# Hybrid decoder layer: SSM and compression products on column tiles, the second gate on VectorE, and the front half as 190 tasks in a new order

## Chip, core and metric

The kernel runs on one core of a Trainium2 chip. The metric is the device time of one execution in microseconds; of several runs the median counts.

## What is computed

A decoder layer over 512 positions of width 1024, all in float32. A modulation vector in six parts (shift, scale and gate of two halves) comes from the condition `c`. The first half projects the normalised, modulated input at once into an attention part and an SSM part. The attention has 8 query heads and 2 key/value heads and three branches: compressed blocks, selected blocks, a window. The second half is a gated feed-forward layer with a causal convolution of three taps.

```python
mod = silu(c) @ w_ada + b_ada
sh1, sc1, gt1, sh2, sc2, gt2 = split(mod, 6)
h = rmsnorm(x, norm1_g) * (1 + sc1) + sh1
zq, zkc, zvc, zks, zvs, zkw, zvw, zg, zs = split(h @ w_in)
# compressed keys and values: 31 blocks of 32 positions, flattened to 2048
kc = gelu((blocks(rope(zkc)) + pe_k) @ w_ck1) @ w_ck2
vc = gelu((blocks(zvc) + pe_v) @ w_cv1) @ w_cv2
o_attn = g0 * softmax(q kc) vc + g1 * selected(q, ks, vs) + g2 * window(q, kw, vw)
y = gelu(Re(C scan(B zs)) + D zs);  y_ssm = y * sigmoid(y @ w_glu + b_glu)
x = x + gt1 * (concat(rmsnorm(o_attn), rmsnorm(y_ssm)) @ w_o)
h = rmsnorm(x, norm2_g) * (1 + sc2) + sh2
a, v = split(conv3(h @ w_up));  x = x + gt2 * ((silu(a) * v) @ w_down)
return rmsnorm(x, normf_g)
```

## The kernel before

The work goes through in this order: modulation and SSM constants; the transposed, modulated input; the SSM projection (`zs`); keys (`zk`) and values (`zv`); the compression; queries (`zq`); the attention, with the SSM's outputs woven in; the output projection (`os`, `oa`); the up projection with the convolution (`up`, 22 pairs of column blocks); the down projection (`dn`).

**Large products** are made of float32 values that are split into a high and a low part of the type fp32r. `mm3` (L111) multiplies high by high, high by low, low by high, which are the lines L112, L113 and L114 of the profile. A weight tile comes by DMA into one of the few `raw` buffers (128x1024, 512 KB); `weights` (L102) has its high part copied (a cast, `cpy`, L55 on ScalarE, L58 on VectorE) and its low part subtracted (L100, on VectorE or GpSimd). When both are done the `raw` buffer is free for the next load. Small products are plain float32; the profile shows two records for each.

**Modulation.** `ada_cols` (L307) computes 256 columns of `silu(c) @ w_ada`: eight products of 256 columns (L314), one on each of four column tiles of 32, twice over, with `csz` as weights, the condition in column 0 of 32 and zeros beside it. A copy brings the four partial rows to a tile `row..`, and two products with ones (L319) turn it into columns. The parts are called `ma`, `mp` (first half), `mg` (gates), `mb`, `mc` (second half). `gate_row` (L330) turns the columns of a gate into a row on all partitions by eight transposes (L336).

**Compression.** `hidden` (L763) builds the blocks `AM` in the tile `mid` and multiplies: 16 steps of 128, two halves of the 256 hidden units, so 32 products for the keys (`w_ck`), then 32 for the values (`w_cv`). The hidden units stand in the output's partitions:

```python
PE.matmul(ph[n][:, :62], r[:, m * 256 + n * 128:m * 256 + (n + 1) * 128],
          AM[:, mm].rearrange("p g n -> p (g n)"), start=mm == 0, stop=mm == 15)
```

Weight tiles go through the `raw` buffers, four for each kind. `compress` (L779) applies gelu and the second product (`co`), once for each kind.

**Attention.** `attend` (L850) goes through 16 units (four blocks of 128 queries, two key heads, two pairs of heads): scores `sc` (L876), masked maximum on VectorE (`mp`, `mx`, L890), exponential on ScalarE (`Ss`, L895), scaling; then the transposes of the compressed probabilities (`pc`, L909), their split `pz`, their product with the compressed values `VC` (L913), and for each key chunk transposes (`p`, L919), split (`pt`, L100) and four products (L929). All products of a unit add up in one bank `pv`.

**What sets the order.** The Python code issues the instructions in a hand-written order; a scheduler that simulates a timeline then orders each engine's queue from it. Each engine works its queue in order. A table `PICK` names for each copy, split and tile the engine or the pool that it goes to (`kn`). All loads are issued by SyncE, in its own queue: a load that waits for its buffer holds up those behind it.

## Time and profile before

| | us |
|---|---|
| three runs | 814.92, 819.27, 820.35 |
| median | 819.27 |
| profiled execution | 818.85 |
| its span | 817.1 |
| TensorE busy | 748.5 (92%) |
| VectorE busy | 469.2 (57%) |
| ScalarE busy | 320.3 (39%) |
| GpSimd busy | 269.2 (33%) |
| mean granted clock of TensorE | 0.936 |

The span is the profiled execution from its first to its last instruction; 1.75 us of that run's own time lie around it. The granted clock is a share of full speed: 1.0 is 2.4 GHz, 0.5 is 1.2 GHz, and a value between is a mean over a stretch. Busy shares are means over stages with different limits.

### The profile page before, as it was taken

The page shows a single profiled execution, that of the slowest core. Times are in us where ns is not written, and L with a number is a line of the kernel's source. Part 1 is how long each engine was busy: PE and PEld are TensorE (multiplying, and loading weights), DVE is VectorE, ACT ScalarE, POOL GpSimd, SP SyncE. Part 2 cuts the span into 40 slices and gives each one's busy share as a digit, 9 for nine tenths or more (in the row PEclk, how much of TensorE's full clock was granted, in tenths as well). Part 3 has the DMA queues.
Part 4 walks back from the last instruction along what each step waited for, and adds up shares of the span by engine and source line. Part 5 has one row for each costly group of instructions (what it writes and reads, how often), then busy time and mean ns, then how long its engine had stood idle before and what let it go on. Part 6 is the DMA issues. An engine that isn't in the chain of part 4 may idle for free.

```text
span 817.1 us, 11305 instructions
## 1 busy us (share of the span) xinstructions
PE 748.5 (92%) x4105; PEld 604.9 (74%) x4105; DVE 469.2 (57%) x1100; ACT 320.3 (39%) x659; POOL 269.2 (33%) x309
## 2 busy tenths in 40 slices
PE   2889989899679889989989999999999999999994
PEld 1469777787456768877779887878778888888883
DVE  5324464348789689778866555455545564132347
ACT  3543243101467767536433233333333322232223
POOL 4899559574522352474321000100000011300003
PEclk9889998759959999999989999999999999999997
DMA  8843226762101005200044133243324323223102
GB/s 298 313 162 105 100 66 209 251 218 73 41 16 23 9 1 222 89 1 1 6 155 155 52 103 109 98 155 103 129 80 153 103 90 114 93 90 104 52 0 103
DMA packets 30458, 86.72 MB, mean 106 GB/s; under 512 B 8295, under 2 KB 8739, under 8 KB 30371
## 3 DMA queue, kind: packets, MB, share of 16 engines
q1 hardware_dynamic: 30403, 86.00, 31.7%
q8 instruction: 32, 0.52, 0.3%
q14 instruction: 23, 0.19, 0.1%
HBM read 82.71 MB, written 2.10 MB: 104 GB/s over the span
## 4 chain that ended last, share of the span: by engine, by line
PE 76%; DVE 12%; ACT 4%; DMA 3%; POOL 2%; issue 2%; SPq 1%; POOLq 0%; DVEq 0%; ACTq 0%
PE up L112 9%; PE up L114 9%; PE up L113 9%; PE dn L114 5%; PE dn L112 5%; PE dn L113 5%; PE hid L776 2%; PE pv L929 2%; DVE Ss L890 2%; PE sc L876 1%; PE eup L113 1%; PE eup L112 1%; DMA adaa<-in_w_ada_dram 1%; PE eup L114 1%; PE p L919 1%
## 5 line engine op out<-in xcount | busy, mean ns | idle before, releaser
L112 PE MATMUL up<-h2h,uup 128*128 128x512 f32 x320 | 128.0, 400 | 0.0
L113 PE MATMUL up<-h2l,uup 128*128 128x512 f32 x320 | 125.8, 393 | 0.0
L114 PE MATMUL up<-h2h,uup 128*128 128x512 f32 x320 | 125.5, 393 | 0.0
L1223 DVE SCALAR_TENSOR_TENSOR us<-up,gt,us 128x511 f32<-128x511 f32 x80 | 59.9, 749 | 58.7 <-ACT us L1219 57.2
L1219 ACT ACTIVATE us<-up,gt 128x512 f32<-128x512 f32 x40 | 31.2, 780 | 109.5 <-PE up L114 109.5
L112 PEld LDWEIGHTS up<-h2h,uup 128*128 128x128 f32 x320 | 60.0, 188 | 15.9 <-ACT us L1219 1.6
L114 PEld LDWEIGHTS up<-h2h,uup 128*128 128x128 f32 x320 | 60.0, 188 | 15.0
L113 PEld LDWEIGHTS up<-h2l,uup 128*128 128x128 f32 x320 | 60.1, 188 | 13.4
L113 PE MATMUL dn<-udn,ghs 128*128 128x512 f32 x176 | 69.6, 396 | 0.0
L112 PE MATMUL dn<-udn,ghs 128*128 128x512 f32 x176 | 69.5, 396 | 0.0
L114 PE MATMUL dn<-udn,ghs 128*128 128x512 f32 x176 | 69.4, 396 | 0.0
L100 DVE TENSOR_TENSOR uup<-rup,uup 128x1024 fp32r<-128x1024 f32 x40 | 48.7, 1221 | 33.8 <-ACT uup L55 33.8
L100 POOL TENSOR_TENSOR udn<-rdn,udn 128x1024 fp32r<-128x1024 f32 x4 | 9.6, 2398 | 151.6 <-DVE udn L58 151.6
L64 POOL TENSOR_SCALAR Ss<-Ss,sm 128x384 f32<-128x384 f32 (+3 forms) x43 | 24.6, 588 | 52.1 <-DVE sm L899 30.1
L55 ACT ACTIVATE uup<-rup 128x1024 fp32r<-128x1024 f32 x36 | 37.8, 1050 | 4.8 <-DMA rup<-in_w_up_dram 3.3
L114 PEld LDWEIGHTS dn<-udn,ghs 128*128 128x128 f32 x176 | 33.1, 188 | 8.1
L112 PEld LDWEIGHTS dn<-udn,ghs 128*128 128x128 f32 x176 | 33.1, 188 | 8.0
L113 PEld LDWEIGHTS dn<-udn,ghs 128*128 128x128 f32 x176 | 33.1, 188 | 7.9
L876 PE MATMUL sc<-KS,QS 128*128 128x288 f32 (+2 forms) x128 | 33.2, 367 | 3.7 <-DVE mp L890 2.6
L929 PE MATMUL pv<-pt,VT 128*128 128x256 f32 x160 | 34.3, 326 | 0.9 <-DVE pt L100 0.9
L895 ACT ACTIVATE Ss<-Ss,mx 128x128 f32<-128x128 f32 (+3 forms) x64 | 35.1, 550 | 0.0
L1276 POOL TENSOR_TENSOR xr<-xr,nf 128x512 f32<-128x512 f32 x4 | 5.7, 1421 | 85.1 <-ACT jz L1275 85.1
(469 smaller groups left out, 1767.9 us busy)
## 6 DMA issues: line engine op xcount, KB each, us to landing
rup<-in_w_up_dram SPq DMA_DIRECT2D x44, 512.0 KB, 3.4
rdn<-in_w_down_dram SPq DMA_DIRECT2D x22, 512.0 KB, 3.3
mid<-in_w_ada_dram SPq DMA_DIRECT2D x16, 512.0 KB, 4.0
adaa<-in_w_ada_dram SPq DMA_DIRECT2D x8, 512.0 KB, 5.6
adap<-in_w_ada_dram SPq DMA_DIRECT2D x8, 512.0 KB, 5.5
adag<-in_w_ada_dram SPq DMA_DIRECT2D x8, 512.0 KB
adab<-in_w_ada_dram SPq DMA_DIRECT2D x7, 512.0 KB, 4.8
xt<-in_x_dram SPq DMA_DIRECT2D x4, 512.0 KB, 5.8
```

The lines of the kernel that those rows point to most:

```text
L55: A.activation(dst, src, AF.Copy, **({} if s is None else {"scale": s}))
L64: P.tensor_scalar(dst, src, s, 1.0, op0=ALU.mult, op1=ALU.mult)
L100: eng.tensor_tensor(out=lo, in0=src, in1=f(hi), op=ALU.subtract)
L112: PE.matmul(ps, w[0], m[0], start=start, stop=False)
L113: PE.matmul(ps, w[0], m[1], start=False, stop=False)
L114: PE.matmul(ps, w[1], m[0], start=False, stop=stop)
L776: PE.matmul(ph[n][:, :62], r[:, m * 256 + n * 128:m * 256 + (n + 1) * 128], AM[:, mm].rearrange("p g n -> p (g n)"), start=mm == 0, stop=m ...
L876: PE.matmul(ps[:, :n], QS[:, h, qs], KS[:, g, x, c0:c0 + n], start=x == 0, stop=x == 1)
L895: A.activation(Sv[:, br, :nk], Sv[:, br, :nk], AF.Exp, bias=mx[:, e, 1 + br:2 + br], scale=0.125, accum_out=sm[:, e, 1 + br:2 + br])
L929: PE.matmul(po[:, :256], VT[:, kc, br, g], pT[:, x, br * 256:(br + 1) * 256], start=False, stop=kc == qt and br == 1 and x == 1)
L1219: A.activation(u_[:, e * n:(e + 1) * n], p, AF.Identity, bias=cv[:, 3, c_:c_ + 1], scale=cv[:, 2, c_:c_ + 1])
L1223: V.scalar_tensor_tensor(o, p[:, :o.shape[1]], cv[:, 2 - d, c_:c_ + 1], o, op0=ALU.mult, op1=ALU.add)
```

## The change

The code of the front half, up to the up projection, is cut into 190 named tasks (`@task`, `@per`), which run in the order of a table `ORDER`. The scores and softmax of an attention unit (`S..`) and its products (`O..`) are tasks of their own. Beside that:

- The hidden products of the compression hold the blocks as weights (64 columns) and move the 256 columns of `w_ck1` or `w_cv1`; keys and values stand on the two column halves of the array and share one bank. Two transposes bring the hidden units back to partitions, gelu and copies run once for both kinds. `w_ck2` and `w_cv2` have a tile of their own.
- The compressed probabilities of a unit are one 128x128 tile with one transpose; their product with `VC` is four products of 128 columns and stands behind the first key chunk's products.
- The second gate (`g2`) and one quarter of `mc` (`c2`) are summed on VectorE: eight operations on 128x256, one scaled by each element of the condition. For the gate the bias is added to one row, and one product with ones adds up the partitions and writes the row to all of them; the columns and transposes are gone.
- `csz` is replaced by a broadcast of `cs` with a scale of 1/32 in the copy.
- The sum of squares of the SSM output is four products of 512 columns on four column tiles, a copy, and four one-column products, where 16 one-column products stood.
- Copies and splits are assigned anew, among them the up projection's: ScalarE 36 to 28 casts, GpSimd 2 to 6 casts and 0 to 8 low halves, VectorE 40 to 32 low halves. Several modulation weights come into other pools than `raw`.

```diff
-    def hidden(kind, w1, pe):
-        AM = mid[:, 2048:3040].rearrange("p (m g n) -> p m g n", m=16, g=2)
...
-                for n in range(2):
-                    PE.matmul(ph[n][:, :62], r[:, m * 256 + n * 128:m * 256 + (n + 1) * 128],
-                              AM[:, mm].rearrange("p g n -> p (g n)"), start=mm == 0, stop=mm == 15)
+    @per("hid", 0, 1, 2, 3)
+    def _(q):
...
+        for w1 in ("w_ck1", "w_cv1"):
+            rr.append(raw(f"{w1}{q}"))
+            nc.sync.dma_start(rr[-1], i[w1][q])
+        for m in range(4):
+            for kind in range(2):
+                PE.matmul(v.ph[kind * 64:(kind + 1) * 64, :256], v.AM[:, kind, q * 4 + m].rearrange("p g n -> p (g n)"),
+                          rr[kind][:, m * 256:(m + 1) * 256], start=v.nh == 1 and m == 0, stop=v.nh == 4 and m == 3)
...
+        if kn("ada_" + name, "PE", "V") == "V":
+            for k in range(KO):
+                w, ck = rr[k // 4][:, (k % 4) * 256:(k % 4 + 1) * 256], cs[:, k:k + 1]
+                if k == 0:
+                    V.tensor_scalar(row, w, ck, None, op0=ALU.mult)
+                else:
+                    V.scalar_tensor_tensor(row, w, ck, row, op0=ALU.mult, op1=ALU.add)
+            return row, ps
...
+    def gate2(jj):
+        row, ps = ada_sums(5120 + jj * 256, f"g2{jj}", raw)
+        c = slice(jj * 256, (jj + 1) * 256)
+        V.tensor_tensor(out=row[0:1], in0=row[0:1], in1=gt2[0:1, 0, c], op=ALU.add)
+        PE.matmul(ps[:, 256:512], bc(ones, (0, 128)), row, start=True, stop=True)
+        cpy(kn(f"e_gc{jj}", "A", "V"), gt2[:, 0, c], ps[:, 256:512])
...
-                for e in range(2):
-                    PE.transpose(pc_[:32, e * 128:(e + 1) * 128], sc[:, e], ident)
-                for x in range(2):
-                    PE.matmul(po[:, :256], VC[:, g], pT[:, x], start=x == 0, stop=False)
+        PE.transpose(pc_[:, :128], scz[ui], ident)
...
+            if kc == 0:
+                for e in range(2):
+                    for x in range(2):
+                        PE.matmul(po[:, e * 128:(e + 1) * 128], VC[:, g, e], pz[:, x], start=False,
+                                  stop=qt == 0 and e == 1 and x == 1)
...
-    for t in range(NT):
-        for ct in range(4):
-            PE.matmul(sq_ps[:, t:t + 1], sqs[:, ct, t * 128:(t + 1) * 128], ones[:, :1], start=ct == 0, stop=ct == 3)
+        for ct in range(4):
+            PE.matmul(sq_ps[32 * ct:32 * ct + 32], bc(ones, (0, 32)), v.sqs[:, ct], start=True, stop=True, tile_position=(0, 32 * ct))
+        sqr = sw("sqr")
+        cpy(kn("e_sqr", "A", "V"), sqr, sq_ps, 1.0 / 32)
+        for t in range(NT):
+            PE.matmul(sq_ps[:, t:t + 1], sqr[:, t * 128:(t + 1) * 128], ones, start=True, stop=True)
```

The order on TensorE in the compression, before: from the last products with the key weights into those with the value weights (`w_cv_1427` to `w_cv_1457` are the four loads).

```order
L776 MATMUL hid_1383<-mid,w_ck_1414 128x62
L776 MATMUL hid_1382<-mid,w_ck_1414 128x62
L776 MATMUL hid_1383<-mid,w_ck_1414 128x62
L314 MATMUL mg_1702<-mid,csz 32x256 x8
L776 MATMUL hid_1425<-mid,w_cv_1427 128x62 x4
L776 MATMUL hid_1425<-mid,w_cv_1437 128x62 x4
L776 MATMUL hid_1425<-mid,w_cv_1447 128x62 x2
L776 MATMUL hid_1426<-mid,w_cv_1427 128x62 x4
L776 MATMUL hid_1426<-mid,w_cv_1437 128x62 x4
L776 MATMUL hid_1426<-mid,w_cv_1447 128x62 x2
```

After: from the column sums of a gate (`mg`) over modulation products of the second half (`mb`) to the first products with the second pair of weights (`w_ck_1423`, `w_cv_1425`).

```order
L394 MATMUL mg_1268<-ones,rowg_1269 128x1 x2
L385 MATMUL mb_1285<-mid,cs 32x256 x4
L385 MATMUL mb_1285<-adab_1283,cs 32x256 x4
L394 MATMUL mb_1285<-ones,rowb_1286 128x1 x2
L744 MATMUL hid<-w_ck_1423,mid 64x256
L385 MATMUL mb_1363<-adab_1359,cs 32x256 x4
L385 MATMUL mb_1363<-adab_1361,cs 32x256 x4
L744 MATMUL hid<-w_cv_1425,mid 64x256
L744 MATMUL hid<-w_ck_1423,mid 64x256
L744 MATMUL hid<-w_cv_1425,mid 64x256
```

The value products no longer form a block of their own, and the products of each pair stand behind the load of that pair.

SyncE's queue at the same place, before (`mid` loads are modulation weights):

```order
L294 DMA mid<-in_w_ada_dram 128x1024 x3
L772 DMA w_ck_1394<-in_w_ck_dram 128x1024
L772 DMA w_ck_1404<-in_w_ck_dram 128x1024
L772 DMA w_ck_1414<-in_w_ck_dram 128x1024
L772 DMA w_cv_1427<-in_w_cv_dram 128x1024
L772 DMA w_cv_1437<-in_w_cv_dram 128x1024
L772 DMA w_cv_1447<-in_w_cv_dram 128x1024
L772 DMA w_cv_1457<-in_w_cv_dram 128x1024
L294 DMA mid<-in_w_ada_dram 128x1024 x2
L106 DMA rinq_1494<-in_w_in_dram 128x1024
L106 DMA rinq_1499<-in_w_in_dram 128x1024
L106 DMA rinq_1504<-in_w_in_dram 128x1024
```

After:

```order
L370 DMA mid<-in_w_ada_dram 128x1024 x6
L741 DMA w_ck_1423<-in_w_ck_dram 128x1024
L741 DMA w_cv_1425<-in_w_cv_dram 128x1024
L370 DMA mid<-in_w_ada_dram 128x1024
L741 DMA w_ck_1435<-in_w_ck_dram 128x1024
L741 DMA w_cv_1437<-in_w_cv_dram 128x1024
L741 DMA w_ck_1447<-in_w_ck_dram 128x1024
L741 DMA w_cv_1449<-in_w_cv_dram 128x1024
L370 DMA mid<-in_w_ada_dram 128x1024 x2
L115 DMA rinq_1488<-in_w_in_dram 128x1024
L115 DMA rinq_1493<-in_w_in_dram 128x1024
L115 DMA rinq_1498<-in_w_in_dram 128x1024
```

Before, the key tiles are requested one behind the other; after, a key and a value tile alternate, the first pair (`w_ck_1411`, `w_cv_1413`) is requested before these rows, and the others wait each for the read of an earlier tile.

TensorE in the attention, before, at the first products of unit 2748 (`pv_2748`; `sc` and `p` belong to its neighbours too):

```order
L929 MATMUL pv_2544<-pt_2558,VT 128x256 x3
L929 MATMUL pv_2544<-pt_2572,VT 128x256 x4
L919 MATMUL p_2757<-ident,Ss 128x128
L919 MATMUL p_2769<-ident,Ss 128x128 x4
L1071 MATMUL yT_2346<-ident,Y_1869 128x64 x8
L876 MATMUL sc_2964<-KS,QS 128x512 x2
L913 MATMUL pv_2748<-pz_2752,VC 128x256 x2
L929 MATMUL pv_2748<-pt_2762,VT 128x256
L876 MATMUL sc_3034<-KS,QS 128x288 x2
```

After, at the first products of unit 2944:

```order
L874 MATMUL pc_2945<-ident,scz_103 128x128
L832 MATMUL sc_3111<-KS,QS 128x512 x2
L832 MATMUL sc_3181<-KS,QS 128x288 x2
L892 MATMUL pv_2944<-pt_2955,VT 128x256 x4
L897 MATMUL pv_2944<-pz_2947,VC 128x128 x4
L892 MATMUL pv_2944<-pt_2971,VT 128x256
L882 MATMUL p_2978<-ident,Ss 128x128 x4
L892 MATMUL pv_2944<-pt_2971,VT 128x256 x3
```

The product with `VC` has moved from the first to the fifth place of its unit.

## Rows read from the trace of the kernel before

**Rows 1.** The page of the profiled execution: the busy time of each engine with its share of the span, and the shares of the chain that ended last.

```profile
PE 748.5 (92%) x4105; PEld 604.9 (74%) x4105; DVE 469.2 (57%) x1100; ACT 320.3 (39%) x659; POOL 269.2 (33%) x309
...
PE 76%; DVE 12%; ACT 4%; DMA 3%; POOL 2%; issue 2%; SPq 1%; POOLq 0%; DVEq 0%; ACTq 0%
```

**Rows 2.** Table of stretches of the span (start and end in us, length, then the busy time and the instructions of each engine, the granted clock of TensorE, the share of the DMA engines and their rate).

```profile
core 0: us, PE busy (x) PEld busy (x) DVE busy (x) ACT busy (x) POOL busy (x), PEclk, DMA share, GB/s
...
144.00:180.00 36.00, 31.88 (x214) 27.92 (x214) 15.51 (x30) 3.31 (x13) 23.09 (x34) 0.63 0.68 224
...
153.00:184.00 31.00, 28.50 (x139) 24.50 (x140) 14.62 (x25) 2.60 (x10) 20.48 (x16) 0.51 0.65 218
...
180.00:260.00 80.00, 67.90 (x458) 50.59 (x456) 64.67 (x263) 37.33 (x129) 33.15 (x30) 0.82 0.19 53
...
260.00:440.00 180.00, 165.46 (x997) 137.87 (x995) 143.61 (x459) 102.31 (x249) 76.21 (x80) 0.94 0.21 71
...
440.00:698.00 258.00, 258.00 (x1197) 207.26 (x1196) 130.97 (x162) 86.45 (x109) 15.46 (x9) 1.00 0.31 104
```

**Rows 3.** Timeline of TensorE in the compression stage (start, length, line, operation, tiles and shape, number of instructions in a row; in brackets the idle time ahead of it and what ended it).

```profile
143.54 1.89 PE L776 MATMUL hid<-mid,w_ck 128*128 128x62 f32 x16
...
146.09 1.07 PE L314 MATMUL mb<-adab,csz 128*32 128x256 f32 x16
...
147.48 2.00 PE L776 MATMUL hid<-mid,w_ck 128*128 128x62 f32 x16 [0.32 <-DMA w_ck<-in_w_ck_dram]
...
149.73 1.98 PE L776 MATMUL hid<-mid,w_ck 128*128 128x62 f32 x16
...
153.83 3.67 PE L776 MATMUL hid<-mid,w_ck 128*128 128x62 f32 x16 [2.12 <-DMA w_ck<-in_w_ck_dram]
...
159.56 13.91 PE L776 MATMUL hid<-mid,w_cv 128*128 128x62 f32 x64 [0.18 <-DVE mid L767]
...
179.49 0.80 PE L112 MATMUL zq<-uinq,hh 128*128 128x512 f32 x1
```

**Rows 4.** DMA issues between 112 and 185 us (size, and the median time from issue to landing).

```profile
w_ck<-in_w_ck_dram SPq DMA_DIRECT2D x4, 512.0 KB, 6.3
...
rinq<-in_w_in_dram SPq DMA_DIRECT2D x4, 512.0 KB, 4.4
```

**Rows 5.** Groups of instructions by line over the whole span: the low halves of the query weights on GpSimd, and the products and transposes of the compressed branch on TensorE (busy time in us, mean of one in ns, and behind the second bar the idle time ahead of them and what ended it).

```profile
L100 POOL TENSOR_TENSOR uinq<-rinq,uinq 128x1024 fp32r<-128x1024 f32 x4 | 10.0, 2489 | 4.2 <-PE hid L776 2.4 <-issue 1.1 <-DVE KS L792 0.7
...
L913 PE MATMUL pv<-pz,VC 32*128 32x256 f32 x32 | 9.2, 355 | 6.5 <-ACT pt L55 2.2 <-DVE pz L100 2.2 <-DVE oT L938 2.1
...
L909 PE MATMUL pc<-ident,sc 128*32 128x128 f32 x32 | 7.4, 321 | 3.3 <-ACT Ss L895 1.9 <-DVE oT L938 0.8 <-DVE sc L900 0.6
```

**Rows 6.** Timeline of TensorE at one of the four second-gate products, among the products of the up projection.

```profile
611.49 0.40 PE L114 MATMUL up<-h2h,uup 128*128 128x512 f32 x1
...
611.81 1.07 PE L314 MATMUL mg<-adag,csz 128*32 128x256 f32 x16
...
613.15 0.40 PE L113 MATMUL up<-h2l,uup 128*128 128x512 f32 x1
```

**Rows 7.** The same further on, at the column sums of that quarter.

```profile
513.00 0.40 PE L114 MATMUL up<-h2h,uup 128*128 128x512 f32 x1
...
513.24 0.50 PE L319 MATMUL mg<-ones,rowg 128*128 128x1 f32 x4
...
513.92 0.40 PE L113 MATMUL up<-h2l,uup 128*128 128x512 f32 x1
```

**Rows 8.** The same between the up and the down projection, at the transposes of the second gate.

```profile
680.01 0.40 PE L114 MATMUL up<-h2h,uup 128*128 128x512 f32 x1
...
680.25 1.95 PE L336 MATMUL gt<-ident,gate 128*128 128x128 f32 x16
...
682.27 0.40 PE L113 MATMUL dn<-udn,ghs 128*128 128x512 f32 x1
```

**Rows 9.** VectorE in the up projection: one f32 operation of each kind from its timeline.

```profile
461.41 0.75 DVE L1223 SCALAR_TENSOR_TENSOR us<-up,gt,us 128x511 f32<-128x511 f32 x1
...
462.08 1.21 DVE L100 TENSOR_TENSOR uup<-rup,uup 128x1024 fp32r<-128x1024 f32 x1
...
460.59 0.69 DVE L58 CAST uup<-rup 128x1024 fp32r<-128x1024 f32 x1
```

**Rows 10.** Timeline of TensorE at the first of the four sums of squares of the SSM output.

```profile
318.96 0.95 PE L1125 MATMUL ssq_s<-ones,ys 128*128 128x1 f32 x8
```

**Rows 11.** Timeline of TensorE between the key and the value projection.

```profile
121.12 1.07 PE L314 MATMUL mb<-adab,csz 128*32 128x256 f32 x16 [2.07 <-DVE gate L328]
...
124.15 0.60 PE L112 MATMUL zv<-uinv,hh 128*128 128x280 f32 x1 [1.96 <-ACT ko L55]
```

**Rows 12.** Timeline of TensorE in the front, up to the first product of the SSM projection.

```profile
34.08 0.63 PE L255 MATMUL ri<-ident,gpt 32*128 32x32 f32 x4 [4.07 <-POOL gpt L215]
...
46.70 0.81 PE L112 MATMUL zs<-uins,hh 128*128 128x512 f32 x1 [3.40 <-ACT hh L55]
```

**Rows 13.** Timeline of ScalarE at the same place.

```profile
44.05 1.04 ACT L55 ACTIVATE uins<-rins 128x1024 fp32r<-128x1024 f32 x1
44.99 2.18 ACT L55 ACTIVATE hh<-scr 128x512 fp32r<-128x512 f32 x4
```

**Rows 14.** What TensorE waited for over the whole span (total us, number of waits, the longest).

```profile
PE pv L913 <- ACT pt L55: 2.2, 1, 2.2
```

More of the change, by code (lines that the diff above doesn't have):

```diff
@@ L307, in ada_cols, with mid_raw, ada_raw @@
-    def ada_cols(n0, name, mk):
-        rr = [ada_dma(n0, name, mk, hf) for hf in range(2)]
-        ps = psum("m" + name, "m" + name, "ms", "pv", "tr", "acc")
+    gate = pc.tile([128, KO], F32, name="gate")
+    n_m = [0]
+    def mid_raw(name):
+        n_m[0] += 1
+        return v.mid[:, (n_m[0] % 2) * 1024:(n_m[0] % 2 + 1) * 1024]
+    def ada_raw(name):
+        k = kn("r_" + name, "raw", "pt", "mid")
+        return raw(name) if k == "raw" else pt([128, 1024], F32, name) if k == "pt" else mid_raw(name)
@@ L465, in tile_layer, with _ @@
+    @task("W")
+    def _():
+        v.W = p2.tile([128, G, 128], F32, tag="wv", name="W")
+        v.scv = p2.tile([128, 2, 2, 4, T, C], F32, tag="x", name="scv")
+    @per("W", *range(8))
+    def _(gq):
+        v.nw = getattr(v, "nw", 0) + 1
+        wb, wt = v.scv[:, v.nw % 2, 0], v.scv[:, v.nw % 2, 1]
         we = kn(f"e_W{gq}", "P", "V")
@@ new lines, in _ @@
+    @task("cv")
+    def _():
+        crow = sw("crow")[:88, 0:256].rearrange("p (x n) -> p x n", x=2)
+        nc.sync.dma_start(crow, i["conv"].rearrange("(x k) p -> k x p", x=2))
+        ps = psum("cv", "cv", "tr", "ms", "pv")
+        for x in range(2):
+            PE.transpose(ps[:, x * 88:(x + 1) * 88], crow[:, x], ident[:88, :88])
+        V.tensor_copy(cv.rearrange("p a b -> p (a b)"), ps[:, :176])
+    for name in ORDER.split():
+        TASKS.pop(name)()
+    assert not TASKS, TASKS
```

1391 lines of the change are left out of this document (605 added, 786 removed).

## Prediction

> **What bounds the kernel now.** The first view is the page: TensorE works 748.5 us of a span of 817.1, and 76% of the chain that ended last is its own work, 12% VectorE's [rows 1]. So what counts is TensorE's time: work taken from it, waits taken from ahead of it, and stretches at half clock. The table of stretches says where each can be had [rows 2]. From 440 to 698 us it is busy 258.00 of 258 at clock 1.00: there a saved microsecond of its work is a microsecond, and nothing else is worth anything. From 144 to 180 us (the compression stage) it is busy 31.88 of 36 at a mean clock of 0.63; the stretch from 153 to 184 us runs at 0.51, which is its lower level (1.2 of 2.4 GHz) nearly throughout. In the attention stages after it (180 to 260 and 260 to 440 us) it sits idle for 12.1 and 14.5 us, with VectorE at 64.67 of 80 and 143.61 of 180: there the question is who waits for whom. The profiled run took 818.85 us, 1.75 beside its span and 0.4 below the median of 819.27; I sum against 818.85 and give the result as the median.
>
> **Compression products (a gain, 8 us).** Before, 64 products (two records each) load 128x128 weights and move 62 columns: 1.89 + 2.00 + 1.98 + 3.67 for the key weights and 13.91 for the value weights, 23.45 us [rows 3]. The same 16 records take 1.89 us at the upper level and 3.67 at the lower. After, 32 products hold 64 columns of blocks and move 256 columns of weights, keys on one column half and values on the other. The trace has no such pair. Nearest is the adaLN product: 16 records, two sets of four products of 256 columns on four column tiles, take 1.07 us, so four products that run beside one another take 0.53 [rows 3]. Sixteen pairs at 0.53 are 8.6 us at the upper level; if the halves did not run side by side they would be 17. I take 8.6: that row has the same number of columns, and shows column tiles running side by side.
>
> That doesn't make the stage 15 us shorter, since it becomes a chain of loads. In the new order only the first pair of weight tiles is requested early. The second pair is requested when the first has been read, the fourth when the second has, and the query weights behind the third and the fourth. A weight tile lands 6.3 us after its issue [rows 4]. First pair 2.1, load 6.3, second pair 2.1, load 6.3, fourth pair 2.1: 18.9 us. Then come the steps from the hidden products to the first query product (activation, second product), which take 6.0 before (159.56 + 13.91 to 179.49 [rows 3]): 24.9 us from the first hidden product to the first query product. A query tile requested behind the third pair is ready by then: it lands in 4.4 [rows 4], and its split takes a cast of 0.7 [rows 9] and a low half of 2.49 on GpSimd [rows 5]. Before, the stage is 143.54 to 179.49, 35.95 us [rows 3]. The other 8.4 us of TensorE's work in that stretch (31.88 less 23.45) are ordered between the pairs and fill the waits in part; I take 3 of them on top, 28 us, a gain of 8. Bounds: if none of that work is covered, 24.9 + 8.4 = 33.3, a gain of 2.6; if the loads land as fast as the query tiles do (4.4), 21.1, a gain of 15. Being a chain of latencies, it keeps the low clock for part of the stretch.
>
> **Second gate on VectorE (a gain, 6.1 us).** Two products of the up projection stand 0.24 us apart [rows 7]. Around one second-gate product, three starts span 1.66 us where two steps would take 0.48, so it costs 1.18 [rows 6]; its column sums cost 0.92 - 0.48 = 0.44 [rows 7]; the transposes at the end cost 2.26 - 0.48 = 1.78 [rows 8]. Four quarters and the end: 4 x 1.62 + 1.78 = 8.3 us. Added on TensorE are four 128x256 products, at most 0.53 each by the row of the adaLN product, 2.1. The net is 6.1, all of it on a full engine. VectorE gets 32 operations on 256 columns, half of a 512-column one of 0.75 us [rows 9], so 12 us, and loses eight low halves of 1.21 us [rows 9], 9.7, to GpSimd, where each costs 2.49 [rows 5], 20 us. VectorE is busy 130.97 of 258 there and GpSimd 15.46 [rows 2], so I cost both at nothing. Without that cover a GpSimd half that comes 2.5 us late stalls TensorE that long, eight times 2.5 or 20 us at worst.
>
> One quarter of the third modulation vector goes to VectorE too: one 1.07 us product less on TensorE, eight operations (3 us) more on VectorE among the key projections. **1.0**, or -2 if VectorE were late there.
>
> The column sums are priced by their rows: 0.44 us for four one-column records [rows 7], 0.95 for eight [rows 10]. The Trainium skill's page TensorEngine Tiling (Array Packing), section Instruction Overhead, has a rule against gains of this kind: each product has some 60 cycles of overhead on TRN2, and one with one column takes as long as one with 60. An estimate from it is 25 ns for such a record, 0.1 us for the four and 0.2 for the eight. By that rule this change would save about 4 us less and come out near 799. The rows show four to five times its figure, with a 128-column weight load for each, and the rows decide.
>
> **Sum of squares (1.8 us).** Four groups of 0.95 us [rows 10] make 3.8. After, four 512-column products on four column tiles (two of the 0.53 steps, 1.07) and four one-column products (0.95): 2.0.
>
> **Compressed branch of the attention (3 us).** The product with the compressed values stood first in each of 16 units and waited 6.5 us in all; its transposes waited 3.3 [rows 5]. It now stands behind the first four key-chunk products, so its own wait for the split probabilities (2.2) is covered. The waits for the chunk's tile (2.2) and for the output bank (2.1) pass to the product that now stands first. I take 3 of 6.5; the ends are 0 and 6.5. Sixteen transposes fewer against 32 narrower products more: between -3.7 us (half of 7.4) and +9.2 (each narrower product as dear as the old, 9.2 for 32 [rows 5]); I take 0, as halves of the same columns.
>
> **The new order of the front half (6 us, 2 given back).** TensorE waits 3.40 us for the split of the normalised input before the first SSM product [rows 12], and ScalarE does a weight cast of 1.04 directly ahead of that split [rows 13]. The order now puts the cast behind, and leaves half the modulation products for later: 3 us, between -1 and 4.4. The wait for GpSimd's chain ahead of it (4.07 [rows 12]) stays. Between key and value projection TensorE waits 2.07 and 1.96 us for work queued behind a block of VectorE operations [rows 11]; the order now puts key products and transposes into that gap: 3 us, between 0 and 4. Both lie ahead of the compression stage, whose first loads must then also come earlier. I give 2 back for that. The reassigned copies I cost at nothing: ScalarE and GpSimd have room in every stretch of [rows 2].
>
> **Sum:** 8 + 6.1 + 1.0 + 1.8 + 3 + 3 + 3 - 2 = 23.9, and 818.85 - 23.9 = **795 us**.
>
> **Rivals.** First, *more*: the loads land as fast as query tiles (15 instead of 8), the full 6.5 of the branch (3.5 more), nothing given back (2), and the shorter waits keep the clock up in the attention stage (0.82 from 180 to 260 with 67.90 us of work; a mean of 0.87 would give 4): 16 or 17 more, 778 us. For it speaks that the low level follows waits; against, that the chain of loads leaves waits of 3 to 4 us itself.
>
> Second, *the early gains are given back*: the loads decide, so stage, branch and order bring nothing together, and only the work taken from TensorE off the chain stays: 6.1 + 1.0 + 1.8 = 9, 810 us. If the narrower products then cost half of their upper bound, 4.6, it is 814.5: no difference to be told. For it speaks the DMA share of 0.68 between 144 and 180 us [rows 2] and the issue order; against, the 12 us of products that are gone at the lower level.
>
> Third, *slower*: scores and products of a unit are now separate steps in an order of their own. If a unit's products follow its softmax too closely, TensorE waits for the softmax in each of 16 units. The longest such wait in the trace is 2.2 us [rows 14]; sixteen are 35 us, 830 us. It decides from 1.5 us a unit (24 / 16), that is when the idle time between 180 and 440 us goes from 26.6 to over 50. For it speaks VectorE's 80% there; against, that the rows of the order read much as before.
>
> **How the numbers follow.** A measurement of this kernel tells about 1% (8 us) from no change. The forecast (784 to 806) has 0.48, *more* (below 784) 0.12, *given back* 0.13 near 810 and 0.15 within 1%, *slower* 0.12. So faster by over 1% is 0.73, within 1% 0.15, slower 0.12. The range, 779 to 816, leaves out the far end of *more* and nearly all of *slower*.
>
> **What would show it.** Right: the hidden products near 9 us at the upper level (17 at the lower), the first query product 25 to 30 us after the first hidden one, waits of TensorE for both kinds of compression weights; the up projection 6 us shorter with TensorE still full; no wait ahead of the compressed-value products. Wrong: TensorE idle in the up projection (GpSimd or VectorE late), the first query product 33 us or more behind the first hidden one, or idle time above 50 us in the attention stages.

## The result and the profile after

The changed kernel takes **788.93 us** (median of four runs, 788.11 to 792.50) against 819.81 for the kernel before on the same chip (median of four, 814.92 to 822.34). The ratio of the means is 0.9639, 95% interval 0.9585 to 0.9693. It is faster by 31 us, 6 us more than forecast and inside the range. The profiled run took 788.76 us with a span of 787.0, so both profiled runs differ by 30.1 us, and that is what the stages below add up to.

From the page of the changed kernel, the lines on the engines and on the chain (beside [rows 1]):

```profile
PE 715.0 (91%) x3947; PEld 582.9 (74%) x3947; DVE 503.1 (64%) x1135; ACT 308.9 (39%) x648; POOL 310.7 (39%) x318
...
PE 66%; DVE 17%; POOL 7%; ACT 4%; issue 4%; DMA 1%; SPq 0%; POOLq 0%; DVEq 0%; ACTq 0%
```

TensorE lost 33.5 us of work, a little more than the whole gain, and its share of the chain fell from 76% to 66%. What remains of the span hangs more on VectorE and GpSimd than before.

The span, cut at the same landmarks in both traces (first `zs` product, first `hid`, first `zq`, last `zq`, last `oa`, first `eup`, first `dn`, last `dn`), in us, with the forecast's terms for each stretch:

| stretch | before | after | change | forecast |
|---|---|---|---|---|
| start to first `zs` | 46.7 | 43.7 | -3.0 | -3 |
| `zs`, `zk`, `zv` | 96.8 | 90.9 | -6.0 | -3 - 1 + 2 |
| compression: first `hid` to first `zq` | 35.95 | 30.46 | -5.5 | -8 |
| `zq` | 27.7 | 29.3 | +1.6 | 0 |
| attention: last `zq` to last `oa` | 205.6 | 193.4 | -12.2 | -3 - 1.8 |
| last `oa` to first `eup` | 6.1 | 10.5 | +4.4 | 0 |
| `eup` and `up` | 263.05 | 256.9 | -6.15 | -6.1 |
| `dn` | 123.35 | 119.8 | -3.55 | 0 |
| after it | 11.8 | 12.1 | +0.3 | 0 |
| sum | 817.1 | 787.0 | -30.1 | -23.9 |

Two neighbours in this table have to be read together: the second profile of the changed kernel (the first experiment below) has 32.1 us for the compression and 27.7 for `zq`, so the same sum, 59.8. Both profiles have the two together 3.9 us shorter than before.

The table of stretches of the changed kernel (columns as in [rows 2]): the compression, `zq`, the attention, the up and the down projection.

```profile
core 0: us, PE busy (x) PEld busy (x) DVE busy (x) ACT busy (x) POOL busy (x), PEclk, DMA share, GB/s
134.56:165.02 30.46, 20.40 (x190) 11.33 (x186) 15.79 (x25) 3.44 (x10) 27.36 (x41) 0.81 0.84 289
165.02:194.60 29.58, 27.92 (x134) 21.61 (x132) 23.57 (x33) 6.49 (x9) 21.59 (x11) 0.90 0.22 71
...
194.30:387.70 193.40, 171.30 (x1148) 142.45 (x1147) 164.56 (x655) 122.01 (x351) 84.67 (x88) 0.90 0.13 40
...
430.80:655.10 224.30, 224.30 (x969) 181.63 (x968) 138.13 (x178) 72.33 (x93) 31.85 (x18) 1.00 0.32 108
655.10:774.90 119.80, 119.80 (x529) 98.91 (x528) 47.21 (x56) 30.17 (x43) 22.57 (x17) 1.00 0.23 80
```

The compression is no longer a full stage: TensorE works 20.40 of 30.46 us (31.8 of 35.95 before). Its timeline there (beside [rows 3]; the whole of it from 134.56 to 165.02, cut):

```profile
134.56 0.43 PE L744 MATMUL hid<-w_ck,mid 128*64 128x256 f32 x1
134.56 0.43 PE L744 MATMUL hid<-w_cv,mid 128*64 128x256 f32 x1
134.82 0.38 PE L744 MATMUL hid<-w_ck,mid 128*64 128x256 f32 x1
134.83 0.38 PE L744 MATMUL hid<-w_cv,mid 128*64 128x256 f32 x1
...
140.47 1.11 PE L744 MATMUL hid<-w_ck,mid 128*64 128x256 f32 x2 [0.61 <-DMA w_ck<-in_w_ck_dram]
...
150.83 0.65 PE L744 MATMUL hid<-w_ck,mid 128*64 128x256 f32 x2 [1.17 <-DMA w_ck<-in_w_ck_dram]
152.11 0.43 PE L744 MATMUL hid<-w_cv,mid 128*64 128x256 f32 x1 [0.63 <-DMA w_cv<-in_w_cv_dram]
...
153.46 0.59 PE L744 MATMUL hid<-w_cv,mid 128*64 128x256 f32 x2
...
161.82 0.69 PE L756 MATMUL hT<-ident,cg 128*128 128x128 f32 x2 [4.94 <-DVE cg L1234]
```

Key and value products start within a hundredth of a microsecond of each other, and a step of the pair is 0.21 to 0.26 us: the column halves do run side by side. The waits for weights are short (2.4 us in all). The longest wait is a new one, 4.94 us for the last VectorE operation of gelu. On VectorE at that place stand a cast of a query weight and that operation, and on GpSimd the low half of the same weight:

```profile
157.37 1.61 DVE L67 CAST uinq<-rinq 128x1024 fp32r<-128x1024 f32 x1
...
159.28 2.49 DVE L1234 SCALAR_TENSOR_TENSOR cg<-cg 128x256 f32<-128x256 f32 x1
```

```profile
159.12 2.37 POOL L109 TENSOR_TENSOR uinq<-rinq,uinq 128x1024 fp32r<-128x1024 f32 x1 [0.68 <-issue]
```

An operation on 256 columns lasts 2.49 us and ends 0.28 us after the GpSimd operation that began ahead of it. The Trainium skill (SBUF — State Buffer, Who interferes with whom) says that a VectorE operation with two inputs from SBUF contends with a GpSimd operation that reads SBUF, over a port pair that one of the two holds as an exclusive lock. The two rows agree; the experiment on the query weights below takes this GpSimd operation away.

### The profile page after: what moved, and what is told of

Its sections match the earlier page's. It is cut to its first block, busy times and chain, and to the rows that moved or that the text cites. A ratio compares the mean times of both kernels' runs of the same rounds, so it can differ in the third digit from the quotient of the medians.

```text
span 787.0 us, 11037 instructions
## 1 busy us (share of the span) xinstructions
PE 715.0 (91%) x3947; PEld 582.9 (74%) x3947; DVE 503.1 (64%) x1135; ACT 308.9 (39%) x648; POOL 310.7 (39%) x318
## 4 chain that ended last, share of the span: by engine, by line
PE 66%; DVE 17%; POOL 7%; ACT 4%; issue 4%; DMA 1%; SPq 0%; POOLq 0%; DVEq 0%; ACTq 0%
PE up L123 9%; PE up L121 9%; PE up L122 9%; PE dn L122 5%; PE dn L123 5%; PE dn L121 5%; DVE Ss L846 2%; PE pv L892 1%; PE eup L123 1%; PE eup L122 1%; PE eup L121 1%; PE y L1004 1%; POOL gpt L200 1%; PE sc L832 1%; PE zs L121 1%
## 5 line engine op out<-in xcount | busy, mean ns | idle before, releaser
L1167 DVE SCALAR_TENSOR_TENSOR us<-up,cst,us 128x511 f32<-128x511 f32 x80 | 59.8, 747 | 63.0 <-ACT us L1165 61.9
L1165 ACT ACTIVATE us<-up,cst 128x512 f32<-128x512 f32 x40 | 31.1, 778 | 107.3 <-PE up L123 107.2
L122 PE MATMUL dn<-udn,ghs 128*128 128x512 f32 x176 | 68.5, 389 | 0.0
L123 PE MATMUL dn<-udn,ghs 128*128 128x512 f32 x176 | 68.5, 389 | 0.0
L121 PE MATMUL dn<-udn,ghs 128*128 128x512 f32 x176 | 68.0, 389 | 0.0
L109 DVE TENSOR_TENSOR uup<-rup,uup 128x1024 fp32r<-128x1024 f32 x32 | 40.9, 1280 | 13.3 <-ACT uup L64 13.1
L71 POOL CAST uup<-rup 128x1024 fp32r<-128x1024 f32 x6 | 7.1, 1186 | 82.6 <-PE up L123 80.4
L109 DVE TENSOR_TENSOR udn<-rdn,udn 128x1024 fp32r<-128x1024 f32 x17 | 22.4, 1316 | 19.0 <-ACT udn L64 11.2
L64 ACT ACTIVATE uup<-rup 128x1024 fp32r<-128x1024 f32 x28 | 29.4, 1049 | 9.4 <-PE up L123 8.1
```

Of the source, the lines that this page charges most:

```text
L64: A.activation(dst, src, AF.Copy, **({} if s is None else {"scale": s}))
L109: eng.tensor_tensor(out=lo, in0=src, in1=f(hi), op=ALU.subtract)
L121: PE.matmul(ps, w[0], m[0], start=start, stop=False)
L122: PE.matmul(ps, w[0], m[1], start=False, stop=False)
L123: PE.matmul(ps, w[1], m[0], start=False, stop=stop)
L1165: A.activation(u_, ps, AF.Identity, bias=cv[:, 3, c_:c_ + 1], scale=cv[:, 2, c_:c_ + 1])
```

## The experiments

The kernel before took 816.0, 817.8, 817.6 and 818.3 us in the four sets of runs, so times of different sets compare to about 2 us; ratios to the kernel before of the same set are given with 95% intervals. Every edit starts from the changed kernel.

**The changed kernel once more.**

> The changed kernel as it is, on the chip of the next three runs, as their point of reference. Both theories on the down projection expect its time to repeat (about 789 us). Theory 'place in memory': the products of the down projection start 0.227 us apart again, as in the first profile of the changed kernel (0.233 before the change). Rival 'this chip or this moment': the distance is another one, and about the same as that of any kernel on this chip.

789.89 us, 0.9671 [0.9633, 0.9709]. This is the base for what follows. Its attention shows something that the first profile alone could not:

```profile
193.90:387.90 194.00, 166.59 (x1148) 138.72 (x1147) 165.64 (x656) 122.03 (x351) 85.33 (x88) 0.94 0.12 40
```

The granted clock was 0.94 there and 0.90 in the first profile, the same products took 4.7 us less, and the stage was 0.6 us longer: TensorE's idle time went from 22.1 to 27.4 us. In this stage TensorE's own speed does not set the length.

**The second gate's sums on TensorE again** (the product with ones stays; four entries go out of the table `PICK`):

```diff
-'ada_g20': 'V', 'ada_g21': 'V', 'ada_g22': 'V', 'ada_g23': 'V',
```

> The second gate's four quarters go back to TensorE's column tiles; the bias, the one product with ones and everything else stay as changed. By the price of the prediction (1.18 us for one such product among those of the up projection) the kernel gets 4.7 us slower, about 794, with TensorE full from 431 us on in both. Rival: VectorE's 32 added operations or GpSimd's added low halves already hold the up projection back; then the return costs less than 2 us, or gains.

794.47 us, 0.9731 [0.9685, 0.9776]: 4.6 us slower, and the attention stays at 193.9. Four products of 1.18 us are 4.7: the price read from [rows 6] holds. The added product with ones reads as follows in the changed kernel:

```profile
487.78 0.39 PE L121 MATMUL up<-h2h,uup 128*128 128x512 f32 x1
488.01 0.59 PE L1146 MATMUL mg<-rowg,ones 128*128 128x256 f32 x2
488.25 0.58 PE L122 MATMUL up<-h2l,uup 128*128 128x512 f32 x1
488.67 0.39 PE L123 MATMUL up<-h2h,uup 128*128 128x512 f32 x1
```

From 488.01 to 488.67 lies one up product (0.23), so the product costs 0.43; the forecast had put it at 0.53 at most.

**The hidden products in the old form**, with the new loads and the new order; the two transposes behind them and their copy go too (not shown):

```diff
-                PE.matmul(v.ph[kind * 64:(kind + 1) * 64, :256], v.AM[:, kind, q * 4 + m]..., rr[kind][:, m * 256:(m + 1) * 256], ...)
+                for n in range(2):
+                    o = (kind * 2 + n) * 64
+                    PE.matmul(v.ph[:, o:o + 64], rr[kind][:, m * 256 + n * 128:m * 256 + (n + 1) * 128], v.AM[:, kind, q * 4 + m]..., ...)
...
```

> The hidden products of the compression in the form from before: 128x128 weights out of the weight tile, 64 columns of blocks moved, twice as many products, no column halves and no transposes behind them; the order of the tasks and the loads stay as changed. Theory 'chain of loads': the stage is set by loads and the steps behind the products, so of the 8 us of work that come back (15 against 7) a part lies under the loads; three of the four weight pairs lie on the chain, 3 x 2 us, less 1.5 for the transposes and their copy: 4 to 5 us slower, about 793. Rival 'hidden anyway': within 1 us. Rival 'work and clock': all 8 us and more, as the products run at the lower clock: 9 or more.

807.76 us, 0.9895 [0.9854, 0.9936], 18 slower. Its timeline and two stretches of its table:

```profile
135.27 0.66 PE L746 MATMUL hid<-mid,w_ck 128*128 128x64 f32 x4
135.77 0.61 PE L746 MATMUL hid<-mid,w_cv 128*128 128x64 f32 x4
...
145.70 1.06 PE L746 MATMUL hid<-mid,w_ck 128*128 128x64 f32 x4
146.55 1.06 PE L746 MATMUL hid<-mid,w_cv 128*128 128x64 f32 x4
...
167.39 1.06 PE L746 MATMUL hid<-mid,w_cv 128*128 128x64 f32 x4
...
177.59 1.12 PE L758 MATMUL co<-cg,cw 128*128 128x64 f32 x4 [5.70 <-DVE cg L1232]
```

```profile
135.27:143.00 7.73, 6.32 (x79) 5.52 (x76) 0.86 (x4) 0.86 (x4) 7.04 (x13) 1.00 0.73 250
143.00:168.00 25.00, 25.00 (x134) 22.50 (x134) 8.08 (x13) 0.77 (x2) 17.24 (x29) 0.51 0.56 193
```

Four records step by 0.45 us at first and by 0.85 after 144 us. TensorE then works 25.00 of 25 us at a clock of 0.51, the lower level, with no wait in it. The clock fell at about 143.6 us, behind waits of 0.56 and 0.85 us; what keeps it low afterwards is not waits, for there are none. First `hid` to first `zq` takes 44.4 us against 30.5 and 32.1. So the expectation of 4 to 5 us, by a chain of loads, falls for this form, and the rival *work and clock* (9 or more) holds: the last weight tile lands at 156.07, and the products go on to 168.45. In the changed kernel it is the other way round: the last tile lands at 152.07 and, in the second profile, at 152.55, and the products that need it start 0.04 us later. There the loads do bound the products, as this row of the second profile shows:

```profile
152.59 0.43 PE L744 MATMUL hid<-w_cv,mid 128*64 128x256 f32 x1 [2.78 <-DMA w_cv<-in_w_cv_dram]
```

The attention is 7 us longer (200.9 us), of which more below, and `zq` 1 to 3 us shorter.

**32 bytes ahead of the normalised inputs**, no other edit:

```diff
+    p2.tile([128, 8], F32, tag="pad", name="pad")
     hh = p2.tile([128, KO, S], F32R, tag="h0", name="hh")
```

> The changed kernel with an unused tile of 32 bytes per partition ahead of the two tiles that hold the gated values (weights of the down projection) and the normalised input (moved in the up projection), so that both start at a multiple of 64 bytes again, as before the change; the weight tiles stay where they are. Theory 'place in memory': the down projection's products start 0.233 us apart again, 528 x 0.0067 = 3.5 us slower, and the up projection's 0.231 instead of 0.2325, 1 us faster: 2.5 us slower in all, about 791.5. Rival: something else in the change (assignment of copies, order) set the distance; then nothing moves.

792.46 us, 0.9702 [0.9664, 0.9739], 2.6 slower. The groups of the down projection's products on the pages of the changed and of the padded kernel (busy us, mean ns):

```profile
L122 PE MATMUL dn<-udn,ghs 128*128 128x512 f32 x176 | 68.5, 389 | 0.0
```

```profile
L122 PE MATMUL dn<-udn,ghs 128*128 128x512 f32 x176 | 69.6, 396 | 0.0
```

396 ns is also the mean in the kernel before. Products stand 0.2334 us apart in it and in the padded kernel, 0.2267 in the changed one; over 528 products that is 3.5 us, the whole change of the down projection, whose products the change leaves as they were. In the changed kernel `ghs` (the gated values) happens to lie at another place: 32 bytes beside a multiple of 64, like the split weights `udn`; before, and with the padding, it lies on a multiple of 64. (These are the addresses that the compiled programs give the tiles; a trace doesn't show them.)

**The same for the weights too**: a padding ahead of the pool moves `udn` and `uup` to multiples of 64, a second one keeps `ghs` 32 beside one.

```diff
+    pc.tile([128, 8], F32, tag="padc", name="padc")
     p2 = ctx.enter_context(tc.tile_pool(name="mid", bufs=1))
...
+    p2.tile([128, 8], F32, tag="pad", name="pad")
     hh = p2.tile([128, KO, S], F32R, tag="h0", name="hh")
```

> Two paddings of 32 bytes a partition: one ahead of the pool with the normalised inputs moves the split weight tiles' successors, the split weights of the up and down projection come to multiples of 64 bytes (they stood 32 beside one in both kernels), and a second one keeps the gated values and the second normalised input where the changed kernel has them (32 beside a multiple). Theory (the place of the held tile decides: the gated values): the down projection's products stay 0.2267 us apart and its length 119.5 us, time within 1 us of the changed kernel. Rival (the place of moved and held tile in relation to each other decides): 0.2334 us and 123 us, 3 us slower; or the up projection (224.3 us) becomes shorter by 1 us or more.

793.68 us, 0.9699 [0.9679, 0.9718]; the page has the slow products again:

```profile
L123 PE MATMUL dn<-udn,ghs 128*128 128x512 f32 x176 | 69.6, 396 | 0.0
```

The theory that the place of `ghs` alone decides falls. The products are fast where both operands lie alike and slow in both mixed cases. That both on multiples of 64 would be fast too was not run. The up projection goes the other way: 224.3 us where `uup` and both parts of the input (`h2h`, `h2l`) lie alike, 223.4 in both padded kernels, where `h2h` lies otherwise and `h2l` alike. No rule for both follows from this.

**Query weights split on VectorE and ScalarE**, GpSimd no longer among them (seven entries go out of `PICK`):

```diff
-'e_inq0': 'P', 'e_inq1': 'P', 'e_inq2': 'P', 'e_inq3': 'P', 'h_inq0': 'V', 'h_inq1': 'V', 'h_inq3': 'V',
```

> The changed kernel with the four query weights split by ScalarE (casts, where three were VectorE's) and VectorE (low halves, where all four were GpSimd's). In the changed kernel the last step of the compression's gelu on VectorE takes 2.49 us beside a GpSimd low half of 2.37, with a cast of 1.61 ahead of it, and TensorE waits 4.9 us for it. Theory 'shared access': VectorE's operation stands still while GpSimd's runs; without it the step takes some 0.4 us, and the first query product comes 2 to 4 us earlier: about 786. Rival 'load': the query tile's own arrival or GpSimd's other work sets the start; then within 1 us. Rival 'VectorE full': four low halves of 1.2 us ahead of the gelu steps make it later, 2 us slower.

791.64 us, 0.9668 [0.9636, 0.9701], no gain. On VectorE the last gelu operation now lasts 1.04 us instead of 2.49, and TensorE's wait for it falls from 4.94 to 1.64:

```profile
160.91 1.04 DVE L1234 SCALAR_TENSOR_TENSOR cg<-cg 128x256 f32<-128x256 f32 x1
```

```profile
162.00 0.69 PE L756 MATMUL hT<-ident,cg 128*128 128x128 f32 x2 [1.64 <-DVE cg L1234]
```

It still doesn't run alone. The GpSimd operation that began ahead of it is now one of the SSM's, and shorter:

```profile
160.54 1.13 POOL L686 TENSOR_TENSOR pra<-A,zu 128x448 f32<-128x448 f32 x1
```

VectorE's operation ends 0.28 us behind it, just as it ended 0.28 us behind the longer one in both profiles of the changed kernel. What it takes without GpSimd is read from operations of the same form, two inputs and 256 columns, elsewhere in the changed kernel: the sums of the second gate (`rowg`, L380) stand in a stretch with little GpSimd work, those of the quarter `c2` (`rowc`) beside a busy GpSimd.

```profile
L380 DVE SCALAR_TENSOR_TENSOR rowg<-adag,cs,rowg 128x256 f32<-128x256 f32 x28 | 14.5, 519 | 1.7 <-DMA adag<-in_w_ada_dram 1.1
L380 DVE SCALAR_TENSOR_TENSOR rowc<-mid,cs,rowc 128x256 f32<-128x256 f32 x7 | 8.0, 1140 | 0.2
```

Of the 28, the 26 with no GpSimd operation beside them take 0.47 to 0.49 us; one that starts 0.08 us behind a GpSimd subtraction takes 1.50 and ends 0.28 us behind it. That settles the stall: the VectorE operation stands still until the GpSimd operation ahead of it is done. The stage is 29.2 us, 1 to 3 shorter. The attention behind it is 202.0 us, 8 longer:

```profile
192.10:394.10 202.00, 176.75 (x1158) 146.44 (x1157) 166.07 (x662) 122.08 (x353) 80.21 (x87) 0.89 0.12 38
```

**Products of a unit directly behind its scores** in the table (three pairs of `S..` and `O..` brought together, `yT1` and `ge3` moved):

> The changed kernel with each attention unit's scores and softmax directly ahead of its products in the table, as in the kernel before; all else as changed. The attention stages (end of the query projection to the last output product) are 12 us shorter in the changed kernel. Theory 'work, not order': that came from products taken away (compressed branch, sum of squares) and moved elsewhere, and TensorE's idle time there is as long as before (27.6 against 26.6); then this run is within 3 us of 789. Rival 'order': the separate tasks brought it, and the stages are 8 us or more longer, about 797.

790.46 us, 0.9659 [0.9629, 0.9688]. It tells little: the scheduler brings out the same queue for TensorE, row for row, and only two rows of VectorE's differ. So the order of the table doesn't set those queues alone, and the rival *order* was not put to the test.

**The compressed-value product first in its unit**, as before:

```diff
+        for e in range(2):
+            for x in range(2):
+                PE.matmul(po[:, e * 128:(e + 1) * 128], VC[:, g, e], pz[:, x], start=x == 0 and e == 0, stop=False)
         for kc in range(qt + 1):
...
-            if kc == 0:
-                for e in range(2):
-                    for x in range(2):
-                        PE.matmul(po[:, e * 128:(e + 1) * 128], VC[:, g, e], pz[:, x], start=False, ...)
```

> The changed kernel with the compressed-value product first in its unit again, as before, in its new form of four narrower products. By the prediction's term 3 us slower (0 to 6.5). Theory from the trace after: the waits ahead of that product have only passed to those that now stand first, as idle time in the attention stages has not fallen; then within 1.5 us of 789.

797.19 us, 0.9737 [0.9707, 0.9767], 5 to 7 slower, the attention 200.9 us. The theory (within 1.5 us) falls. The size lies at the upper end of the term's 0 to 6.5, but not for the term's reason: the product waits 1.1 us in all here. The groups of the changed kernel and then of this one (last numbers: idle time ahead, and what ended it):

```profile
L897 PE MATMUL pv<-pz,VC 128*128 128x128 f32 x64 | 10.1, 286 | 0.0
L874 PE MATMUL pc<-ident,scz 128*128 128x128 f32 x16 | 5.1, 329 | 3.2 <-DVE scz L856 1.6 <-DVE oT L906 0.8 <-DVE QS L796 0.7
```

```profile
L879 PE MATMUL pv<-pz,VC 128*128 128x128 f32 x64 | 12.0, 311 | 1.1 <-ACT pt L64 0.5 <-ACT pz L64 0.2 <-DVE oT L904 0.2
L874 PE MATMUL pc<-ident,scz 128*128 128x128 f32 x16 | 5.2, 340 | 6.9 <-DVE scz L856 2.1 <-DVE oT L904 2.0 <-ACT Ss L851 1.5
```

**One quarter of `mc` and the squares back on TensorE**, together and each alone:

```diff
-'ada_c2': 'V',
...
-        for ct in range(4):
-            PE.matmul(sq_ps[32 * ct:32 * ct + 32], bc(ones, (0, 32)), v.sqs[:, ct], start=True, stop=True, tile_position=(0, 32 * ct))
-        sqr = sw("sqr")
-        cpy(kn("e_sqr", "A", "V"), sqr, sq_ps, 1.0 / 32)
         for t in range(NT):
-            PE.matmul(sq_ps[:, t:t + 1], sqr[:, t * 128:(t + 1) * 128], ones, start=True, stop=True)
+            for ct in range(4):
+                PE.matmul(sq_ps[:, t:t + 1], v.sqs[:, ct, t * 128:(t + 1) * 128], ones[:, :1], start=ct == 0, stop=ct == 3)
```

> The changed kernel with two parts undone together: the one quarter of the third modulation vector back on TensorE's column tiles, and the sum of squares of the SSM output as 16 one-column products again. By the prediction's terms 1.0 + 1.8 = 2.8 us slower, about 792. Rival: both lie in stretches where TensorE waits anyway; then less than 1 us.

811.75 us, 0.9913 [0.9877, 0.9949]: 20 to 22 us slower where the two terms make 2.8.

> Only the sum of squares of the SSM output goes back: 16 one-column products instead of four of 512 columns on column tiles, a copy and four one-column products. Theory (the loss of the run with both parts undone lies in the attention, where the scheduler orders TensorE anew as soon as the squares change): most of the 22 us comes back with this part alone, 803 to 812, with the attention (last value projection of the queries to the output projection's end) 8 to 18 us longer than 194 and its granted clock below 0.87 in the first 84 us. Rival (the terms of the sum hold when each part is undone alone): 1.8 us, 791 to 793.

794.04 us, 0.9703 [0.9685, 0.9720]: 2.6 us by the ratios, with 1.8 for the term. The theory (803 to 812) falls. In the changed kernel the squares read 1.06 and four times about 0.28 us, 2.2 for the 3.8 of [rows 10]:

```profile
301.58 1.06 PE L1064 MATMUL ssq_s<-ys,ones 128*32 128x512 f32 x8
...
304.08 0.28 PE L1068 MATMUL ssq_s<-ones,sqr 128*128 128x1 f32 x2
```

> Only the quarter of mc goes back from VectorE to TensorE. Theory (the loss lies with the squares): 1 to 3 us slower than the changed kernel, 790 to 793, the query projection at most 1 us later. Rival (the loss begins ahead of the queries, by the load and the buffer that this quarter takes, and the clock then stays low through the attention): 800 or more, with the first query product 3 us or more later and the granted clock under 0.83 in the first 80 us of the attention.

807.98 us, 0.9870 [0.9832, 0.9908]: 16 us slower for one product of 1.07 us. The profiled run is the fastest of its four (802.95). The theory that the loss lies with the squares falls. The first query product comes 1 to 2 us later; the loss is 3 to 5 us in `zq` (32.6), with a wait for the compressed keys that the changed kernel doesn't have, and 9 us in the attention:

```profile
171.51 0.80 PE L121 MATMUL zq<-uinq,hh 128*128 128x512 f32 x1 [3.31 <-DVE KS L764]
```

```profile
200.00:402.90 202.90, 174.76 (x1152) 145.94 (x1151) 164.94 (x661) 121.87 (x353) 82.55 (x87) 0.87 0.12 38
```

**The same quarter on TensorE, but late**, beside the other quarters:

```diff
-... L1 s2 U3 ... VV6 b3 s0 S00 ...
+... L1 U3 ... VV6 b3 s2 s0 S00 ...
```

> The quarter of mc goes back to TensorE as in the run before, but its task stands behind the query projection, beside the other quarters, and no longer among the key projections; its loads go through the same tile. Theory (what costs there is the place: with the quarter among the key projections the key copies on VectorE come late, TensorE waits for them ahead of the queries, and VectorE goes late into the attention): the wait of the first query products for VectorE's KS (3.3 us) is gone, attention within 3 us of 194, time 789 to 793. Rival (the order of the attention that the table fixes fits one front half alone; the scheduler's queue for TensorE and VectorE there comes out differently with any change ahead of it): 797 to 810, with the granted clock in the first 80 us of the attention below 0.85.

805.78 us, 0.9844 [0.9815, 0.9874]. The wait for the keys is gone, as the theory said, but the time stays: compression 36.1 us, of which a shorter `zq` (25.5) gives most back, attention 207.3, with a clock of 0.81 from 200 to 283 us. The rival holds.

**What these runs have in common** is read from the compiled order of two queues: VectorE's from the first row of a unit's maximum (`mx`) to the last of its splits (`pt`), 628 rows in the changed kernel, and TensorE's from the first scores to the last products of the units, 929 rows. The table has how many of these rows do not fit into the longest order that a kernel shares with the changed one, beside the attention's length.

| kernel | VectorE rows moved | TensorE rows moved | attention, us |
|---|---|---|---|
| changed, twice | 0 | 0 | 193.4, 194.0 |
| padded, twice | 0 | 0 | 196.3, 194.9 |
| second gate's sums on TensorE | 0 | 0 | 193.9 |
| products behind scores | 1 | 0 | 194.8 |
| squares back | 6 | 10 | 197.6 |
| compressed product first | 182 | 272 | 200.9 |
| quarter of `mc` back | 239 | 336 | 202.9 |
| the same and squares | 240 | 335 | 210.2 |
| the same, late | 184 | 180 | 207.3 |
| query weights without GpSimd | 211 | 179 | 202.0 |
| old hidden products | 249 | 253 | 200.9 |

VectorE is busy 164 to 168 us of the attention in every one of these kernels. The seven profiles with both queues as in the changed kernel, or nearly so, take 193 to 198 us; the six with queues that the scheduler sorted anew take 201 to 210, whatever was edited. In the seven TensorE is busy 166 to 172 us of the stage and idle 22 to 28, in the six 173 to 184 and 25 to 29. That the order of the queues is the cause is argued from this table, not shown, and which of the two queues it would be stays open: they moved together in every run. No kernel of these beats the changed one beyond the 2 us that sets differ by.

## Why the prediction was right, and where its steps were not

**The sum was right within 6 us of 30, by terms that missed on both sides.** That is in part luck: the attention gave 7.4 us more than its terms and the down projection 3.5 without any, against 2.5 less in the compression and 4.4 lost ahead of the up projection. Held to size: the wait ahead of the first SSM product (-3 forecast, -3.0; the first `zs` product follows without a wait), the key/value gap (-3; the stretch from the first `zv` product to the first `hid` is 3.8 shorter and begins without a wait), the up projection (-6.1 against -6.15 with the early products; TensorE full, as [rows 2] had it, so a saved microsecond was one; VectorE's 32 operations took 15.9 us there instead of 12, and it had the room), the squares (-1.8 against 2.6 undone).

**Compression (8, was 5.5).** The price of a pair of products, 0.53 us, was a little high: four pairs step through in 1.7 to 1.9 us. The chain of loads held: a load took 6.5 us by the median, near the 6.3 of [rows 4], and first to last hidden product took 19.5 us, 21.5 in the second profile, where 18.9 and 3 stood in the sum. The last pair started as its second tile landed. The waits of 3 to 4 us that were to show it did not come: TensorE waited 2.4 us for all loads, 3.3 in the second profile, since the modulation products ordered between the pairs filled the time. The DMA engines were at 0.84 of the stage (0.69 before). What failed is the term behind it: 6.0 us from the hidden products to the first query product, copied from [rows 3], became 11.0 (10.7 in the second profile), because a gelu operation stood behind a cast and then beside a GpSimd operation. GpSimd's 2.49 us halves were in [rows 5]; that they lengthen VectorE's operations was not looked for. The low level was foreseen as following waits; in the run with the old form it set in behind waits of 0.56 and 0.85 us, but stayed for 25 us with TensorE full.

**Compressed branch (3, cannot be credited).** The mechanism went as described: the product with the compressed values has no wait ahead of it in 64 records. But TensorE's idle time in the attention went from 23.6 us only to 22.1, so the waits passed to others, and the narrower products were not free: 9.2 us became 10.1, while the transposes' 7.4 became 5.1, so the two together are 1.4 us less. The run that undoes it sorted both queues anew and prices nothing by itself.

**Attention (4.8 forecast, was 12.2).** TensorE is busy 10.7 us less and idle 1.5 less. Part of the work is only elsewhere: `mb3` and `mc` products now run ahead of the queries and with them, 2.5 us, and 1.9 us of transposes now stand behind `oa`. With the squares (1.6 by their rows) and the 1.4 of the branch that leaves some 5 us, an estimate from these rows. Both queues are new there, for which the forecast had no term; whether that brought the 5 us stays open. The *slower* rival asked for over 50 us of idle time; it is 22 to 29 in all profiles.

**Missed outside the terms.** The down projection's 3.5 us came from where a tile happened to lie. The gap between attention and up projection grew by 4.4 us: 1.9 by the transposes that moved into it, the rest by idle time of TensorE, of which the longest wait, 3.49 us (2.31 before), is for a VectorE operation ahead of the last transposes:

```profile
397.35 0.69 PE L941 MATMUL h<-ident,xn 128*128 128x128 f32 x2 [3.49 <-DVE xn L69]
```

That is gain given back at a place that the forecast didn't name; it takes the 4 us by which the front came out better than forecast (9.0 for 5).

**The quarter `c2` (1.0)** is the term whose undoing differs most: 16 us. The step "a product less, eight VectorE operations more" had VectorE's part too low: the eight operations took 9.4 us instead of 3, as they ran beside a busy GpSimd (the `rowc` rows above). What moving them did to the queues behind wasn't priced at all. The rival *given back* was refuted by the compression (3.9 with `zq`) and the attention (12.2).

## What to carry to other kernels

Where a planner sorts the queues, undoing one part need not price that part: first compare the queues of the stages behind it, and read the price only from runs in which they kept their order. On a stretch where TensorE is full, prices added up from the starts of neighbouring products hold to a few tenths of a microsecond. When a stage becomes shorter, look at the step behind it for an operation that will now stand beside a long one on a neighbouring engine. A price taken from a stretch where that neighbour rests doesn't hold where it works: 0.48 us against 1.14 for one form of operation here.

## What the runs showed of the hardware that was not expected

- Products of 512 columns step by 0.2267 or 0.2334 us at full clock by the place of their two operands, 32 bytes being enough to change it (three kernels with the slow step, all others with the fast one in `dn`); in `up` the effect is smaller and of the other sign (224.3 against 223.4 us).
- A VectorE operation with two inputs from SBUF on 256 columns took 0.48 us alone; started behind a GpSimd operation, it ended 0.28 us after that one, whatever its length (2.49 us beside 2.37, 1.04 beside 1.13, 1.50 beside 1.29). Operations of the same form with one input from a product's output (`rope`, from `zq`) took 0.41 us beside GpSimd too.
- TensorE ran at the lower clock level for 25 us in which it was never idle (old hidden products, 134 records, mostly with 128x128 weights and 64 columns). It had fallen there behind waits of 0.56 and 0.85 us. The new form kept a mean of 0.81 with a third of the stage idle.
